# A ScalarE copy between the parts of the last pair's chain, in the halved feed-forward stages

## The chip, the cores and the metric

The kernel runs on one core of one Trainium2 chip. The metric is the device time of one execution in microseconds (us). Five engines work side by side and wait for each other through semaphores: TensorE (PE in the profile; PEld is its weight load) multiplies matrices, VectorE (DVE) and ScalarE (ACT) work on elements, GpSimd (POOL) and SyncE (SP) here mostly issue transfers (DMA). Each engine takes its own instructions strictly in the order in which they stand in its queue.

## The reference, cut to what matters

One decoder layer over 512 tokens of width 1024: a feed-forward half-step, a mixing stage with two kinds of attention, and a second feed-forward half-step. The change lies in the two half-steps alone:

```python
D_MODEL = 1024; SEQ = 512; D_FF = 2816

def swiglu_ffn(x, g, w_gate, w_up, w_down):
    h = rms_norm(x, g)
    return (jax.nn.silu(h @ w_gate) * (h @ w_up)) @ w_down

x = x + 0.5 * swiglu_ffn(x, ffn1_norm, ffn1_w_gate, ffn1_w_up, ffn1_w_down)
...                                   # attention, gates, output projection
x = x + 0.5 * swiglu_ffn(x, ffn2_norm, ffn2_w_gate, ffn2_w_up, ffn2_w_down)
```

All of it is in float32.

## The kernel before, in words

**Precision.** Every float32 operand is held as two parts, a high one (a ScalarE cast) and a low one (a VectorE subtraction of the high part from the source). One product is three matmuls (`mm3`, lines 147 to 149): high weights by high data, high weights by low data, low weights by high data. For a weight tile, `split_w` makes the parts: ScalarE casts `wh` on line 116, VectorE subtracts `wl` on line 123. So the third matmul of the first `mm3` of a product is the first that needs `wl`.

**Steps.** `ffn` writes its work as a list of steps. A step has weights to load, a `split` that makes their two parts, and a `run` that multiplies. The main loop takes the steps one after the other. At step i it first calls `look_ahead(i)`, which loads and splits the weights of the steps up to i + 2 (so at step i it is step i + 2 that is newly split), then empties the list `later`, and then calls `run` of step i. Between `ordered[0]` and `ordered[1]` the order of the instructions on ScalarE, VectorE and GpSimd is the order in which the Python code writes them; TensorE's order is written out for the whole kernel.

**Pairs.** The 22 tiles of 128 columns of the hidden width D_FF go in groups, (0, 4), (4, 10), (10, 16), (16, 22). From the fifth tile on, two tiles make a pair, and a pair's gate and up products are made by a scheme of seven products of half-size blocks in place of eight (steps A, s1, s2, b, s3, s4, d in `pair_steps`), at the price of sums of blocks made by VectorE. When the last product of a pair is done, `finish` puts a closure `begin` into `later`: the Silu (line 397), the product with it (398), and then what the down product needs.

**Halved down products.** In the groups of `HALVED` (two in the first half-step, three in the second: five places in the program) the down product has seven half-size products as well. Its moving operands are the blocks `b1`, `ta`, `tb`, `b2`, each as a high and a low part. `combine_first` makes `b1` and the first half of `ta` from the pair's first tile; `combine_second` (lines 260 to 276) makes the rest from the second tile `u`: `fb` and `fa` are VectorE's sums, `split_halves` casts (245) and subtracts (247). Of the last pair of a group this is done at once, the high parts of `tb`'s first half and `b2` first (267, 272), and it falls into the first steps of the down product. This is the chain of the title.

**The seven down steps** (`halved_steps`, twice per group, for two halves of the output) are, in TensorE's order: `run_1` (bank dA from `b1`; ScalarE then copies dA into dB, line 521), `run_5` (dD from `ta`'s first half), `run_6` (adds `tb`'s first half onto dB), `run_2` (adds `b2`'s first half onto dA), `run_7` (`ta`'s second half onto dB), `run_3` (dC), `run_4` (dB). Each has 18 matmuls of 256 columns: six `mm3`, and the two of the last pair come last, so that only the 13th to the 18th matmul of a product need the last pair's blocks. dD goes out through ScalarE copies `e` (513), in the very last group through VectorE (506).

Of the kernel before, what the change touches and what calls it, by code (L numbers as in the profile page):

```python
# [12 lines left out]
F32 = mybir.dt.float32  # L13
F32R = mybir.dt.float32r
AF = mybir.ActivationFunctionType
OP = mybir.AluOpType
# [4 lines left out]
T = 512  # L21
# [26 lines left out]
HT = T // 2  # L48
# [6 lines left out]
def tile_hybrid_layer(ctx: ExitStack, tc: tile.TileContext, a: dict):  # L55
    nc = tc.nc
    V, S, G, PE = nc.vector, nc.scalar, nc.gpsimd, nc.tensor
# [12 lines left out]
    def tmp_tile(name):  # L70
        return tmp.tile([P, T], F32, tag="t", name=name)
# [33 lines left out]
    first = None  # L105
# [93 lines left out]
    def ffn(n, nxt, parts=lambda d: [slice(0, T)]):  # L199
        wg, wu, wp, wd, wh_ = (a[f"w_{nm}{n}"] for nm in ("gate", "up", "pair", "down", "halves"))  # L200
        gi = 0 if n == 1 else 2
        with tc.tile_pool(name=f"ffn{n}", bufs=1) as ap, tc.tile_pool(name=f"halves{n}", bufs=1) as hp:
# [12 lines left out]
            def split_act(f, u, late):  # L215

                h, l = act_tiles(f)
                S.copy(h, u)
                if late:
                    S.mul(l, h.bitcast(F32), -1.0)  # L220
                    G.dma_start(l, u, accum_op=OP.add)
                else:
                    V.tensor_sub(l, u, h.bitcast(F32))

            def halves(q):
                lo = next(lo for lo, hi in GROUPS if lo <= 2 * q < hi)
                j = q - lo // 2
                if q not in act:
                    tiles = [ap.tile([P, 2 * T], F32R, tag=f"a{j}{i}", name=f"a{i}") for i in "hl"]
                    ta = stream(6 + j, F32R, "ta") if j < 2 else ap.tile([P, 2 * T], F32R, tag="a2t", name="ta")  # L230
                    b1 = ap.tile([P, T], F32R, tag=f"a{j}b", name="b1")
                    act[q] = dict(b2=[t[:, :T] for t in tiles], tb=[t[:, T:] for t in tiles],
                                  ta=[ta[:, :T], ta[:, T:]], b1=[b1[:, :HT], b1[:, HT:]])
                return act[q]

            def split_late(q, nm, src, cols):
                h, l = (t[:, cols] for t in halves(q)[nm])
                S.copy(h, src)
                S.mul(l, h.bitcast(F32), -1.0)
                G.dma_start(l, src, accum_op=OP.add)  # L240

            def split_halves(q, *which):
                t = halves(q)
                for nm, src, cols in which:
                    S.copy(t[nm][0][:, cols], src[:, cols])
                for nm, src, cols in which:
                    V.tensor_sub(t[nm][1][:, cols], src[:, cols], t[nm][0][:, cols].bitcast(F32))
# [12 lines left out]
            def combine_second(q, u, last):  # L260
                t = halves(q)
                fa, fb = t["fa"], tmp_tile("fb")
                first, second = slice(0, HT), slice(HT, T)
                V.scalar_tensor_tensor(fb[:, first], fa[:, first], -1.0, u[:, second], op0=OP.mult, op1=OP.subtract)
                if last:
                    for nm, src, cols in (("tb", fb, first), ("b2", u, slice(0, T))):
                        S.copy(t[nm][0][:, cols], src[:, cols])
                V.tensor_sub(fa[:, second], u[:, second], t["u1"][:, second])
                V.scalar_tensor_tensor(fb[:, second], fb[:, first], -1.0, u[:, first], op0=OP.mult, op1=OP.subtract)
                if last:  # L270
                    for nm, src, cols in (("tb", fb, first), ("b2", u, slice(0, T))):
                        V.tensor_sub(t[nm][1][:, cols], src[:, cols], t[nm][0][:, cols].bitcast(F32))
                    split_halves(q, ("ta", fa, second), ("tb", fb, second))
                    return []
                return [lambda nm=nm, src=src: split_late(q, nm, src, slice(0, T))
                        for nm, src in (("b2", u), ("tb", fb), ("ta", fa))]

            def activate(f, pg, pu, rb):
# [98 lines left out]
            def pair_steps(q, last, halved):  # L377
# [4 lines left out]
                t, raw = {}, {}  # L382
# [11 lines left out]
                def finish(f, gu):  # L394

                    def begin():
                        S.activation(gu[:, 0], gu[:, 0], AF.Silu)
                        V.tensor_mul(gu[:, 1], gu[:, 1], gu[:, 0])
                        if not halved:
                            return [lambda: split_act(f, gu[:, 1], not last)]  # L400
                        return (combine_second if f % 2 else combine_first)(q, gu[:, 1], last)

                    later.append((begin, last))

                def gu_tile():
                    return stream(2 + next(gu_at), F32, "gu").rearrange("p (m t) -> p m t", m=2)
# [41 lines left out]
                def run_s4(w):  # L448
                    product(t["C"], w, moving("b2", 1), False)
                    V.tensor_add(t["gu1"][:, :, HT:], view(t["C"]), view(t["p5"]))  # L450
                    finish(2 * q, t["gu1"])

                def run_d(w):
                    product(t["B"], w, moving("tb", 1), False)
                    S.mul(t["gu2"][:, :, :HT], view(t["B"]), -1.0)
                    finish(2 * q + 1, t["gu2"])
# [140 lines left out]
                return run  # L597

            steps = []
            later = deque()  # L600
            ordered = [None, None]
            gu_at = cycle(range(4))
            for lo, hi in GROUPS:
# [27 lines left out]
            def load():  # L631
                i, (key, f, src) = queue.pop(0)

                tag = max(sorted(free), key=lambda z: used[::-1].index(z) if z in used else len(used))
                free.remove(tag)
                used.append(tag)
                t = ap.tile([P, 1024], F32, tag=tag, name=tag) if tag in ("rd", "re", "rf") else raw_tile(tag)
                steps[i].raw[key] = t, tag
                nc.sync.dma_start(t[:, :f * P].rearrange("p (n m) -> p n m", n=f) if f else t, src)

            def look_ahead(i):

                for j in range(i, min(i + 1 + steps[i].ahead, len(steps))):
                    if j not in ws:
                        while queue and queue[0][0] <= j:
                            load()
                        ws[j] = steps[j].split()
                        free.update(steps[j].raw[z][1] for z in steps[j].frees)
                while queue and queue[0][0] <= i + 6 and free:
                    load()  # L650
# [4 lines left out]
            for i, st in enumerate(steps):  # L655
                if i == ordered[0]:
                    in_order.enter_context(tc.manual_schedule(engines={
                        mybir.EngineType.Activation, mybir.EngineType.DVE, mybir.EngineType.Pool}))
                look_ahead(i)
                while later:  # L660
                    item, urgent = later.popleft()
                    later.extendleft((z, urgent) for z in reversed(item() or ()))
                    if not urgent and i < ordered[1]:
                        break
                if i == ordered[1]:
                    in_order.close()
                st.run(ws[i])
                if rbs and combos:
                    for _ in range(2):
                        if next(combos, "end") == "end":  # L670
                            combos = None
                            free.add("rd")
                            break
# [3 lines left out]
    first = [[], []]  # L677
# [22 lines left out]
    gq = const.tile([P, 2], F32, name="gq")  # L700
    V.tensor_scalar(gq, hg[:, 0:2], -0.125, None, op0=OP.mult)
    ffn(1, lambda d, cols: (prep(d, 1), add_square(d)))


    with (tc.tile_pool(name="mix", bufs=1) as mp, ExitStack() as att_ctx,
# [255 lines left out]
        def dsa_keys():  # L961
            for t in range(NT):
                r = qk_scale(sd[0][:, t, 0], 1)
                V.tensor_scalar(sd[0][:, t], sd[0][:, t], r[:, 0:1], None, op0=OP.mult)
                S.copy(dvv[:, t, 0:64], sg[:, t, 0:64])
                V.tensor_sub(dvv[:, t, 64:128], sg[:, t, 0:64], dvv[:, t, 0:64].bitcast(F32))
            yield
            evac_split(transposed(lambda t: sd[0][:, t].rearrange("p a d -> p (a d)"), "ps_dk"), hg[:, 3:4], dkh, dkl)
# [80 lines left out]
        later = [dsa_keys(), forget()]  # L1049
# [146 lines left out]
        for g in range(2 * H):  # L1196
            q, k, bias = nq, nk, nb
# [69 lines left out]


    ffn(2, lambda d, cols: nc.sync.dma_start(a["y"][:, d, cols], x[d][:, cols]),
        lambda d: [slice(0, T)] if d < KD - 1 else [slice(0, T // 2), slice(T // 2, T)])  # L1270

# [79 lines left out]
```

## Time and profile before

| | |
|---|---|
| median of 3 runs | 1094.66 us (1093.4 to 1096.35) |
| the profiled execution, its own time | 1093.11 us |
| its span, from the first to the last instruction | 1091.4 us |
| what lies around the span | 1.71 us |
| PE busy | 1061.4 us, 97% of the span |
| PE weight loads | 980.7 us, 90% |
| DVE busy | 838.8 us, 77% |
| ACT busy | 662.4 us, 61% |
| POOL busy | 242.5 us, 22% |
| mean clock granted to TensorE | 0.993 of full speed |

How to read the rows that follow. A row of a timeline has the start and the duration in us, the engine, the line of the kernel, the operation, what it writes and reads, its shapes, and in brackets how long the engine was idle before it and what it waited for. Names stand without their numbers: `s` is a sum of weight blocks, `wh` and `wl` the two parts of a weight tile, `ah` and `al` those of the blocks `tb` and `b2`, `gu` a pair's gate and up result, `ra` to `rf` raw weight tiles. A row of waits has the total wait in us, how often, and the longest. A matmul's duration in a row is longer than the distance between the starts of two, since they overlap.

### The profile page before, as it was taken

The numbers are of one execution on the slowest core, as the hardware profiler recorded it, in microseconds if no ns is written. First come the engines' busy times: TensorE is split into PE (matmuls) and PEld (weight loads), VectorE is DVE, ScalarE is ACT, GpSimd is POOL, SyncE is SP. The second block draws the span as 40 slices with busy tenths as digits, with TensorE's granted clock in tenths as the row PEclk, the third lists the DMA queues.
The fourth block names the chain that finished last, engine by engine and source line by source line (L and its number), as shares of the span: only waits on it lengthen the run. The fifth ranks groups of instructions, "written<-read, shape, count | busy, mean of one in ns | idle before, by whom it ended". The sixth has DMA issues, their size and how long they took to land.

```text
span 1091.4 us, 19211 instructions
## 1 busy us (share of the span) xinstructions
PE 1061.4 (97%) x7330; PEld 980.7 (90%) x7330; DVE 838.8 (77%) x1375; ACT 662.4 (61%) x1096; POOL 242.5 (22%) x311
## 2 busy tenths in 40 slices
PE   8999999999999999999999999999999999999998
PEld 6889999999998889999878788788889999999998
DVE  6887888877867579986776676854877878787886
ACT  6736765755665665576866666444637655855763
POOL 1100210111000024267776661000101110110110
PEclk9999999999999999999999999999999999999999
DMA  7544754657442267723323321633555654656553
GB/s 234 144 154 108 158 137 140 139 142 183 109 107 89 78 145 173 214 89 106 79 60 115 116 68 49 196 100 82 116 158 125 139 158 122 144 135 173 121 121 108
DMA packets 55133, 140.04 MB, mean 128 GB/s; under 512 B 6392, under 2 KB 13944, under 8 KB 55040
## 3 DMA queue, kind: packets, MB, share of 16 engines
q1 hardware_dynamic: 39888, 110.22, 33.8%
q0 software_dynamic: 15008, 28.32, 14.6%
q8 instruction: 58, 0.95, 0.4%
q10 hardware_dynamic: 144, 0.26, 0.1%
q14 instruction: 35, 0.29, 0.1%
HBM read 104.94 MB, written 3.42 MB: 99 GB/s over the span
## 4 chain that ended last, share of the span: by engine, by line
PE 69%; DVE 11%; issue 8%; ACT 6%; POOL 4%; DMA 2%; SPq 0%; DVEq 0%; POOLq 0%; ACTq 0%
PE pB L148 4%; PE pB L147 4%; PE pB L149 4%; PE pA L148 3%; PE pA L147 3%; PE pA L149 3%; PE ps_f L147 3%; PE ps_f L148 3%; PE ps_f L149 3%; PE dB L147 2%; PE dB L148 2%; PE dB L149 2%; PE pD L148 2%; PE pD L149 2%; PE pD L147 2%
## 5 line engine op out<-in xcount | busy, mean ns | idle before, releaser
L123 DVE TENSOR_TENSOR wl<-s,wh 128x1024 fp32r<-128x1024 f32 (+1 forms) x84 | 94.6, 1126 | 39.5 <-ACT wh L116 39.5
L116 ACT CAST wh<-s 128x1024 fp32r<-128x1024 f32 (+1 forms) x84 | 81.8, 973 | 61.9 <-PE pC L148 31.1
L147 PE MATMUL ps_t<-wh,xh 128*128 128x256 f32 (+1 forms) x288 | 80.6, 280 | 0.0
L149 PE MATMUL pB<-tbh,wl 128*128 128x256 f32 x288 | 80.4, 279 | 0.0
L147 PE MATMUL pB<-tbh,wh 128*128 128x256 f32 x288 | 80.4, 279 | 0.0
L148 PE MATMUL pB<-tbl,wh 128*128 128x256 f32 x288 | 80.4, 279 | 0.0
L148 PE MATMUL ps_t<-wl,xh 128*128 128x256 f32 (+1 forms) x288 | 80.3, 279 | 0.0
L149 PE MATMUL ps_t<-wh,xl 128*128 128x256 f32 (+1 forms) x288 | 80.3, 279 | 0.0
L147 PE MATMUL ps_f<-xh,wh 128*128 128x512 f32 x152 | 60.5, 398 | 0.0
L149 PE MATMUL ps_f<-xh,wl 128*128 128x512 f32 x152 | 59.6, 392 | 0.0
L148 PE MATMUL ps_f<-xl,wh 128*128 128x512 f32 x152 | 59.6, 392 | 0.0
L147 PEld LDWEIGHTS ps_t<-wh,xh 128*128 128x128 f32 x288 | 54.3, 188 | 0.5
L148 PEld LDWEIGHTS ps_t<-wl,xh 128*128 128x128 f32 x288 | 54.3, 188 | 0.5
L1062 ACT ACTIVATE p<-p,mn 128x512 f32<-128x512 f32 (+1 forms) x64 | 36.0, 562 | 30.6 <-DVE mn L1060 30.1
L149 PEld LDWEIGHTS ps_t<-wh,xl 128*128 128x128 f32 x288 | 54.3, 188 | 0.0
L147 PEld LDWEIGHTS pB<-tbh,wh 128*128 128x128 f32 x288 | 54.1, 188 | 0.0
L149 PEld LDWEIGHTS pB<-tbh,wl 128*128 128x128 f32 x288 | 54.1, 188 | 0.0
L148 PEld LDWEIGHTS pB<-tbl,wh 128*128 128x128 f32 x288 | 54.1, 188 | 0.0
L240 POOL DMA_DIRECT2D b<-gu x10 | 8.7, 866 | 197.9 <-DVE rf L417 100.7
L1064 POOL TENSOR_SCALAR p<-p,rs 128x512 f32<-128x512 f32 (+1 forms) x64 | 39.1, 614 | 59.6 <-DVE rs L1063 59.2
L147 PE MATMUL dB<-ah,wh 128*128 128x256 f32 x120 | 37.0, 308 | 11.7 <-ACT dB L521 11.7
L515 POOL DMA_DIRECT2D xa<-e x16 | 19.1, 1193 | 124.8 <-ACT wh L116 115.8
(399 smaller groups left out, 4152.0 us busy)
## 6 DMA issues: line engine op xcount, KB each, us to landing
ra<-in_w_pair_dram SPq DMA_DIRECT2D x15, 512.0 KB, 3.7
rc<-in_w_pair_dram SPq DMA_DIRECT2D x15, 512.0 KB, 4.0
re<-in_w_pair_dram SPq DMA_DIRECT2D x12, 512.0 KB, 4.0
rf<-in_w_pair_dram SPq DMA_DIRECT2D x12, 512.0 KB, 3.7
rb<-in_w_pair_dram SPq DMA_DIRECT2D x12, 512.0 KB, 3.6
xa<-e POOLq DMA_DIRECT2D x16, 256.0 KB, 3.8
rd<-in_w_halves_dram SPq DMA_DIRECT2D x10, 384.0 KB, 3.8
al<-gu POOLq DMA_DIRECT2D x14, 256.0 KB, 5.3
```

The lines of the kernel that those rows point to most:

```text
L116: S.copy(wh[:, :f], raw[:, :f])
L123: V.tensor_sub(wl[:, :f], raw[:, :f], wh[:, :f].bitcast(F32))
L147: PE.matmul(out, lh, rh, start=start, stop=False, **more)
L148: PE.matmul(out, lh, rl, start=False, stop=False, **more)
L149: PE.matmul(out, ll, rh, start=False, stop=stop, **more)
L240: G.dma_start(l, src, accum_op=OP.add)
L515: return lambda: G.dma_start(xa[:, d:d + 2, half * HT:half * HT + HT], e, accum_op=OP.add)
L1062: S.activation(p, p, AF.Exp, bias=mn, scale=-1.0, accum_out=rs)
L1064: G.tensor_scalar(p, p, rs, 1.0, op0=OP.mult, op1=OP.mult)
```

## The change

For the second tile of the last pair of a halved group, `begin` goes into a new list `before`, which the loop empties ahead of `look_ahead`. `combine_second` does then only the Silu, its product and the first half of `fb`, and puts the closure `soon` into another new list, `after`, which the loop empties behind `run`. `soon` splits the first half of `tb` and the whole of `b2`, makes the second halves of `fa` and `fb`, and puts their split into `later`, where the next step takes it, after its own `look_ahead`. So the chain is in three parts: ahead of the first step's weight split, behind the first step's `run` (and so behind the copy from dA to dB), and behind the second step's weight split. No instruction is added or taken away; GpSimd's and SyncE's queues have the same rows in the same order, and so has TensorE's.

```diff
@@ combine_second
                 t = halves(q)
                 fa, fb = t["fa"], tmp_tile("fb")
-                first, second = slice(0, HT), slice(HT, T)
+                first, second, both = slice(0, HT), slice(HT, T), slice(0, T)
                 V.scalar_tensor_tensor(fb[:, first], fa[:, first], -1.0, u[:, second], op0=OP.mult, op1=OP.subtract)
+
+                def others():
+                    V.tensor_sub(fa[:, second], u[:, second], t["u1"][:, second])
+                    V.scalar_tensor_tensor(fb[:, second], fb[:, first], -1.0, u[:, first], op0=OP.mult, op1=OP.subtract)
+
+                def soon():
+                    split_halves(q, ("tb", fb, first), ("b2", u, both))
+                    others()
+                    later.append((lambda: split_halves(q, ("ta", fa, second), ("tb", fb, second)), True))
+
                 if last:
-                    for nm, src, cols in (("tb", fb, first), ("b2", u, slice(0, T))):
-                        S.copy(t[nm][0][:, cols], src[:, cols])
-                V.tensor_sub(fa[:, second], u[:, second], t["u1"][:, second])
-                V.scalar_tensor_tensor(fb[:, second], fb[:, first], -1.0, u[:, first], op0=OP.mult, op1=OP.subtract)
-                if last:
-                    for nm, src, cols in (("tb", fb, first), ("b2", u, slice(0, T))):
-                        V.tensor_sub(t[nm][1][:, cols], src[:, cols], t[nm][0][:, cols].bitcast(F32))
-                    split_halves(q, ("ta", fa, second), ("tb", fb, second))
+                    after.append(soon)
                     return []
-                return [lambda nm=nm, src=src: split_late(q, nm, src, slice(0, T))
+                others()
+                return [lambda nm=nm, src=src: split_late(q, nm, src, both)
                         for nm, src in (("b2", u), ("tb", fb), ("ta", fa))]
@@ finish, in pair_steps
-                    later.append((begin, last))
+                    if last and halved and f % 2:
+                        before.append(begin)
+                    else:
+                        later.append((begin, last))
@@ the list of steps
-            later = deque()
+            before, later, after = deque(), deque(), deque()
@@ the main loop
+                while before:
+                    before.popleft()()
                 look_ahead(i)
                 while later:
...
                 st.run(ws[i])
+                while after:
+                    after.popleft()()
```

ScalarE, at the first of the five places (the others read alike): the last pair's Silu, the weight casts of the down product's third and fourth step (`wh<-s_1448`, `wh<-rf`), the casts of the last pair's blocks, and the copy from dA to dB. Before:

```order
L455 ACTIVATE gu<-pB 128x2x256
L116 CAST wh<-s_1448 128x768
L397 ACTIVATE gu<-gu 128x512
L267 CAST ah<-fb 128x256
L267 CAST ah<-gu 128x512
L245 CAST ta<-fa 128x256
L245 CAST ah<-fb 128x256
L521 COPY dB<-dA 128x512
L116 CAST wh<-rf 128x768
```

and of the change (its line numbers are 4 to 7 higher here):

```order
L462 ACTIVATE gu<-pB 128x2x256
L401 ACTIVATE gu<-gu 128x512
L116 CAST wh<-s_1448 128x768
L528 COPY dB<-dA 128x512
L245 CAST ah<-fb 128x256
L245 CAST ah<-gu 128x512
L116 CAST wh<-rf 128x768
L245 CAST ta<-fa 128x256
L245 CAST ah<-fb 128x256
```

The Silu stands ahead of the weight cast, the copy ahead of the four casts of blocks, and the second weight cast ahead of the last two of them.

VectorE at the same place, from the Silu's product (`gu<-gu`) to the low part of the fourth step's weights (`wl<-rf`) and the block subtractions. Before:

```order
L123 TENSOR_TENSOR wl<-s_1448,wh 128x768
L398 TENSOR_TENSOR gu<-gu 128x512
L264 SCALAR_TENSOR_TENSOR fb<-fa,gu 128x256
L268 TENSOR_TENSOR fa<-gu 128x256
L269 SCALAR_TENSOR_TENSOR fb<-fb,gu 128x256
L272 TENSOR_TENSOR al<-fb,ah 128x256
L272 TENSOR_TENSOR al<-gu,ah 128x512
L247 TENSOR_TENSOR ta<-fa,ta 128x256
L247 TENSOR_TENSOR al<-fb,ah 128x256
L477 TENSOR_TENSOR s_1448<-s_1448,rf 128x768
L123 TENSOR_TENSOR wl<-rf,wh 128x768
```

and of the change:

```order
L402 TENSOR_TENSOR gu<-gu 128x512
L264 SCALAR_TENSOR_TENSOR fb<-fa,gu 128x256
L123 TENSOR_TENSOR wl<-s_1448,wh 128x768
L247 TENSOR_TENSOR al<-fb,ah 128x256
L247 TENSOR_TENSOR al<-gu,ah 128x512
L267 TENSOR_TENSOR fa<-gu 128x256
L268 SCALAR_TENSOR_TENSOR fb<-fb,gu 128x256
L484 TENSOR_TENSOR s_1448<-s_1448,rf 128x768
L123 TENSOR_TENSOR wl<-rf,wh 128x768
L247 TENSOR_TENSOR ta<-fa,ta 128x256
L247 TENSOR_TENSOR al<-fb,ah 128x256
```

The low part of the third step's weights moved behind the Silu's product and the first `fb`; the second halves of `fa` and `fb` moved behind the first two block subtractions, and the last two block subtractions behind the fourth step's weights.

## The prediction

> **What bounds the kernel now.** I read the page first, for the busiest engine, and then who that engine waits for.
>
> ```profile
> PE 1061.4 (97%) x7330; PEld 980.7 (90%) x7330; DVE 838.8 (77%) x1375; ACT 662.4 (61%) x1096; POOL 242.5 (22%) x311
> ```
>
> TensorE is busy for 97% of the span, so only its idle time and its pace are to be had. The view of waits, for TensorE alone, begins:
>
> ```profile
> PE dB L147 <- ACT dB L521: 11.7, 5, 2.3
> PE pt L1071 <- POOL p L1064: 2.0, 3, 1.2
> ```
>
> The first row is six times the second: five stops of up to 2.3 us, before the first matmul into dB, for ScalarE's copy of dA into dB. They are the five places of the change. I take the second of them; TensorE's timeline there:
>
> ```profile
> 231.17 0.27 PE L149 MATMUL dD<-ta,wl 128*128 128x256 f32 x1
> 233.79 0.43 PE L147 MATMUL dB<-ah,wh 128*128 128x256 f32 x1 [2.34 <-ACT dB L521]
> ...
> 237.54 0.28 PE L147 MATMUL dA<-ah,wh 128*128 128x256 f32 x1
> ...
> 239.65 0.28 PE L147 MATMUL dB<-ta,wh 128*128 128x256 f32 x1
> ```
>
> The dA product (18 matmuls) takes 239.65 - 237.54 = 2.11 us, 0.117 a matmul. So dB could have begun at 231.17 + 0.12 = 231.29, and the stop costs 233.79 - 231.29 = 2.50 us (the row's 2.34 counts from the end of the last matmul). The dB product behind it takes 237.54 - 233.79 = 3.75 us, which is 1.64 more than the same 18 matmuls in dA. The granted clock says why (columns: window, its length, busy us of PE, PEld, DVE, ACT, POOL, then the clock):
>
> ```profile
> 138.42:141.83 3.41, 2.21 (x19) 2.00 (x18) 2.96 (x6) 1.85 (x5) 0.00 (x0) 1.00 0.37 112
> 230.58:233.99 3.41, 1.07 (x9) 0.86 (x8) 3.38 (x10) 2.27 (x6) 0.00 (x0) 1.00 0.02 5
> 233.99:237.40 3.41, 3.41 (x17) 3.41 (x17) 2.74 (x4) 2.20 (x4) 0.00 (x0) 0.50 0.18 25
> 527.54:530.95 3.41, 1.83 (x15) 1.39 (x14) 3.02 (x6) 2.81 (x5) 3.33 (x8) 1.00 0.98 251
> 530.95:534.36 3.41, 3.41 (x29) 3.33 (x28) 2.95 (x10) 3.11 (x8) 3.32 (x4) 1.00 0.45 105
> ```
>
> After a window in which TensorE was idle for 3.41 - 1.07 = 2.34 us it ran 3.41 us at half speed. The first place (first row), whose stop is cut by the edge of a window into pieces of about 1.2, has no such stretch (its rows stand below), nor has the window behind the worst one elsewhere (the last two rows: 1.58 idle, then 1.00).
>
> **The change, part by part.** No instruction is added; what moves is the order on ScalarE and VectorE. So I set the new order with the old rows' durations. ScalarE before, at this place:
>
> ```profile
> 228.31 0.59 ACT L455 ACTIVATE gu<-pB 128x512 f32<-128x512 f32 x1
> 228.80 0.82 ACT L116 CAST wh<-s 128x768 fp32r<-128x768 f32 x1
> 229.52 0.63 ACT L397 ACTIVATE gu<-gu 128x512 f32<-128x512 f32 x1
> 231.72 0.40 ACT L267 CAST ah<-fb 128x256 fp32r<-128x256 f32 x1 [1.56 <-DVE fb L264]
> 232.03 0.61 ACT L267 CAST ah<-gu 128x512 fp32r<-128x512 f32 x1
> 232.55 0.40 ACT L245 CAST ta<-fa 128x256 fp32r<-128x256 f32 x1
> ...
> 233.16 0.57 ACT L521 COPY dB<-dA 128x512 f32<-128x512 f32 x1
> 233.67 0.82 ACT L116 CAST wh<-rf 128x768 fp32r<-128x768 f32 x1
> ```
>
> and VectorE:
>
> ```profile
> 229.66 0.96 DVE L123 TENSOR_TENSOR wl<-s,wh 128x768 fp32r<-128x768 f32 x1 [0.80 <-ACT wh L116]
> 230.53 0.69 DVE L398 TENSOR_TENSOR gu<-gu 128x512 f32<-128x512 f32 x1
> 231.26 0.42 DVE L264 SCALAR_TENSOR_TENSOR fb<-fa,gu 128x256 f32<-128x256 f32 x1
> 231.60 0.42 DVE L268 TENSOR_TENSOR fa<-gu 128x256 f32<-128x256 f32 x1
> ...
> 232.67 0.69 DVE L272 TENSOR_TENSOR al<-gu,ah 128x512 fp32r<-128x512 f32 x1
> 233.28 0.42 DVE L247 TENSOR_TENSOR ta<-fa,ta 128x256 fp32r<-128x256 f32 x1
> ...
> 233.95 0.95 DVE L477 TENSOR_TENSOR s<-s,rf 128x768 f32<-128x768 f32 x1
> 234.82 0.95 DVE L123 TENSOR_TENSOR wl<-rf,wh 128x768 fp32r<-128x768 f32 x1
> ```
>
> A result is taken up 0.04 us after it is done (product ends at 231.22, `fb` starts at 231.26); an independent instruction starts a little before its forerunner ends: 0.72 us behind a weight cast, 0.31 behind a cast of 256, 0.52 behind one of 512, 0.34 behind a VectorE sum of 256, 0.61 behind one of 512, 0.87 behind one of 768.
>
> *The Silu goes ahead of the weight cast.* It starts at 228.31 + 0.59 + 0.04 = 228.94 and ends at 229.57. VectorE, idle for 0.80 us just there, takes the product at 229.61 (to 230.30) and `fb` at 230.34 (to 230.76): 0.92 us earlier than before.
>
> *The weight cast, and the copy behind it.* The cast starts 0.53 behind the Silu, at 229.47, and ends at 230.29; the copy follows at 229.47 + 0.72 = 230.19 and ends at 230.76, 2.97 us earlier than before and 0.53 ahead of the slot of 231.29 that TensorE has for dB. dA must be done by then; its last matmul stands before the 18 of dD, so about 2.1 us ahead of 231.29. The stop for the copy is gone.
>
> *What is late next, first.* `wl<-s` now stands behind product and `fb`: 230.34 + 0.34 = 230.68 to 231.64, where it ended at 230.62. The third matmul of dB (231.29 + 0.23 = 231.52) needs it; with 0.06 from an end to a matmul (copy's end 233.73, dB 233.79) that is 231.70, a stop of **0.18 us**. The last pair's blocks are needed only by the 13th matmul (232.9): `ah<-fb` is cast at 230.80, once `fb` is done, and `al<-fb` follows `wl<-s` at 231.55, done at 231.97. About 0.9 us of older pairs' matmuls cover it; without that cover TensorE would wait as long as it now does for `al`.
>
> *What is late next, second.* VectorE goes on: `al<-gu` at 231.89, `fa` at 232.50, `fb` at 232.84, the sum `s` at 233.17, `wl<-rf` at 234.04, done at 234.99. That is only 0.78 us earlier than before. dA now begins at 231.29 + 0.18 + 2.11 = 233.57, its third matmul is due at 233.80 and must wait for 234.99 + 0.06 = 235.05: a new stop of **1.25 us**. Between the ends "hidden" (0) and "`wl<-rf` as late as before" (2.03) I take 1.25, since each step of that chain has its row. Before, the slow dB product had covered this tile.
>
> *The step after.* ScalarE's casts of the second halves wait for `fa` and `fb` (232.96 and 233.30), two `e` copies and the cast of `rd` follow, as before:
>
> ```profile
> 234.40 1.07 ACT L513 ACTIVATE e<-dD 128x512 f32<-128x512 f32 x2
> 235.37 0.82 ACT L116 CAST wh<-rd 128x768 fp32r<-128x768 f32 x1
> ```
>
> With 0.30 + 0.97 + 0.82 behind 233.30 the cast ends at 235.39; VectorE reaches `wl<-rd` at 234.04 + 0.87 + 2 x 0.34 = 235.59 and ends at 236.55. The next product (`ta`'s second half) begins at 233.57 + 2.11 + 1.25 = 236.93 and needs it at 237.16: hidden by 0.6 us. Its start was 239.65, so this place gains **2.72 us**. Behind it VectorE and ScalarE wait for TensorE again, and all that follows, transfers with it, moves as one; no load or accumulating transfer changes its place in its queue.
>
> *The clock.* The new stops leave about 1.1 us between modelled ends of matmuls, less than the 1.58 that brought no slow stretch. I take full speed. The Trainium skill bears on this ("TensorE: Matmul & The Clock Gate", section "What's actually happening"): the clock falls to half after at least one idle window of about 3.4 us and is given back after a busy one. The half-speed stretch of 3.41 us agrees with its window; the condition does not, since 2.34 us of idleness in a window were enough here. By the page alone the stops could not be the cause, and the slow stretches would stay.
>
> *The other places.* dB's old start and the next product's old start:
>
> ```profile
> 142.97 0.39 PE L147 MATMUL dB<-ah,wh 128*128 128x256 f32 x1 [2.34 <-ACT dB L521]
> ...
> 147.27 0.28 PE L147 MATMUL dB<-ta,wh 128*128 128x256 f32 x1
> ...
> 875.81 0.58 PE L147 MATMUL dB<-ah,wh 128*128 128x256 f32 x1 [2.33 <-ACT dB L521]
> ...
> 881.61 0.28 PE L147 MATMUL dB<-ta,wh 128*128 128x256 f32 x1
> ...
> 968.13 0.58 PE L147 MATMUL dB<-ah,wh 128*128 128x256 f32 x1 [2.34 <-ACT dB L521]
> ...
> 973.85 0.28 PE L147 MATMUL dB<-ta,wh 128*128 128x256 f32 x1
> ...
> 1060.36 0.58 PE L147 MATMUL dB<-ah,wh 128*128 128x256 f32 x1 [2.35 <-ACT dB L521]
> ...
> 1066.09 0.28 PE L147 MATMUL dB<-ta,wh 128*128 128x256 f32 x1
> ```
>
> At place two the new start is 236.93, 3.14 behind dB's old one; the same chain puts the others at 146.11, 878.95, 971.27 and 1063.50: gains of 1.16 (no slow stretch there before), 2.66, 2.58 and 2.59. The last place has one more piece on VectorE:
>
> ```profile
> 1062.26 1.28 DVE L506 SCALAR_TENSOR_TENSOR xa<-dD,xa 128x512 f32<-128x512 f32 x2
> 1063.46 0.95 DVE L123 TENSOR_TENSOR wl<-rd,wh 128x768 fp32r<-128x768 f32 x1
> ```
>
> These 1.20 us stand ahead of `wl<-rd`, which then ends 1.20 us later than at place two, 0.64 too late (237.75 + 0.06 against 237.16): 2.59 - 0.64 = 1.95.
>
> **Sum:** 1.16 + 2.72 + 2.66 + 2.58 + 1.95 = 11.07 us. The profiled execution took 1093.11 us, span 1091.4 and 1.71 around it, and would take 1082.0. It lies 1.55 below the median of the runs; from the median I predict 1094.66 - 11.07 = **1083.6 us**.
>
> **The rivals.**
>
> *The half speed stays* at four places, whether the shorter stops still bring it or something else did. For it: the first place shows that the condition depends on where a window begins. Against it: every slow stretch followed a window with over 2 us idle, and none came elsewhere. The excess of dB's products over 2.11 us is worth 1.64 + 1.58 + 1.50 + 1.51 = 6.23 (next product's start less dB's, less 4.22); the gain falls to 4.84, 1089.8 us. By the page's rule it comes out here too.
>
> *VectorE's chain is not earlier:* `wl<-rf` ends at 235.77 as before. For it: VectorE has no idle time from 230.53 to there. Against it: the 0.80 us before `wl<-s` is taken away. 0.78 less at each place: gain 7.2, 1087.5.
>
> *No new stop:* everything is saved, 5 x 2.50 + 6.23, less 5 x 0.18: 17.8, 1076.9. Against it stands the row of `wl<-rf`; it would have to be done 1.2 us sooner.
>
> *Slower:* one stop has become two, and idle time in two neighbouring windows drops the clock in both. From about 1 us idle per window on, each place would pay the stops (1.43, once 0.64 more) and two slow stretches of about 1.56: 7.8 + 15.6 = 23.4 against 5 x 2.50 + 6.23 = 18.7 now, 4.7 slower, 1099.4. Against it: 1.58 us idle in one window did nothing.
>
> **How the numbers follow.** Forecast 0.67, VectorE not earlier 0.11, half speed stays 0.11, no new stop 0.07, slower 0.04. The forecast's own range is 1081 to 1086 (a quarter of a microsecond at each stop, and the spread of the runs). To hold eight in ten the range takes in the second and third case: 1079.5 to 1090. A measurement of this kernel tells 0.3%, 3.3 us, from no change. The half-speed case lies near that edge, and with a late VectorE inside it: of its 0.11 I count 0.07 as the same. Faster 0.67 + 0.11 + 0.04 + 0.07 = 0.89, same 0.07, slower 0.04.
>
> **What would show it.** Right: the wait of dB's L147 for ScalarE's copy is gone from TensorE's waits; in its place stand waits of dA's L149 for `wl` of about 1.1 us, five times, with `wl` ending 0.8 us earlier against the pair's last product; the clock is 1.00 behind all five places; the dB product takes 2.1 to 2.3 us. Wrong: half-speed windows at the same places; a stop at dB's 13th matmul for `ah` or `al`; a new stop at the `ta` product at places one to four; or a copy that starts later than dD ends.

## The result, and the profile after

The changed kernel takes 1083.57 us (median of 4 runs, 1082.64 to 1084.4) against 1094.2 before (4 runs), a ratio of 0.990 with the interval 0.9881 to 0.9918. It is faster by 1.0%, and 1083.6 was forecast. In a second comparison it took 1082.8 against 1093.47, ratio 0.9902 (0.9885 to 0.9918). The profiled execution took 1084.4 us, its span is 1082.6.

TensorE's waits in the profile after:

```profile
PE dA L149 <- DVE wl L123: 4.9, 5, 1.0
PE pt L1082 <- DVE kl L737: 1.8, 3, 1.1
...
PE dB L149 <- DVE wl L123: 0.4, 1, 0.4
```

The 11.7 us for ScalarE's copy are gone. In their place stand five waits of 1.0 us for the low part of the fourth step's weights, and one of 0.4 at the last place. TensorE's timeline at place two, which answers to the rows of before:

```profile
231.99 0.28 PE L149 MATMUL dD<-ta,wl 128*128 128x256 f32 x1
232.11 0.28 PE L147 MATMUL dB<-ah,wh 128*128 128x256 f32 x1
232.22 0.28 PE L148 MATMUL dB<-al,wh 128*128 128x256 f32 x1
232.43 0.38 PE L149 MATMUL dB<-ah,wl 128*128 128x256 f32 x1
...
234.40 0.28 PE L147 MATMUL dA<-ah,wh 128*128 128x256 f32 x1
234.52 0.27 PE L148 MATMUL dA<-al,wh 128*128 128x256 f32 x1
235.78 0.39 PE L149 MATMUL dA<-ah,wl 128*128 128x256 f32 x1 [0.98 <-DVE wl L123]
...
237.76 0.28 PE L147 MATMUL dB<-ta,wh 128*128 128x256 f32 x1
```

ScalarE's copy there:

```profile
230.96 0.58 ACT L528 COPY dB<-dA 128x512 f32<-128x512 f32 x1
```

It ends at 231.54, 0.57 us before dB's first matmul at 232.11. dB follows dD without a stop; its third matmul comes 0.21 us behind the second where 0.12 is usual; dA's third comes 1.26 behind the second. From dD's last matmul to the `ta` product it is 237.76 - 231.99 = 5.77 us, before 239.65 - 231.17 = 8.48: a gain of 2.71. Why dA waits stands on VectorE:

```profile
230.36 0.69 DVE L402 TENSOR_TENSOR gu<-gu 128x512 f32<-128x512 f32 x1 [0.73 <-ACT gu L401]
231.09 0.43 DVE L264 SCALAR_TENSOR_TENSOR fb<-fa,gu 128x256 f32<-128x256 f32 x1
231.43 0.95 DVE L123 TENSOR_TENSOR wl<-s,wh 128x768 fp32r<-128x768 f32 x1
...
233.91 0.95 DVE L484 TENSOR_TENSOR s<-s,rf 128x768 f32<-128x768 f32 x1
234.78 0.95 DVE L123 TENSOR_TENSOR wl<-rf,wh 128x768 fp32r<-128x768 f32 x1
```

From the Silu's product to the start of `wl<-rf` VectorE works without a break, 4.42 us, and `wl<-rf` ends at 235.73, 0.05 before dA's third matmul. The windows of 3.41 us around it (PE busy is the second column, the clock the third from the end):

```profile
234.42:237.83 3.41, 2.43 (x21) 2.23 (x20) 3.26 (x6) 2.96 (x6) 0.00 (x0) 1.00 0.24 66
237.83:241.25 3.42, 3.42 (x31) 3.42 (x30) 3.21 (x5) 1.68 (x2) 0.00 (x0) 1.00 0.69 219
...
428.98:432.39 3.41, 3.41 (x28) 3.24 (x27) 3.38 (x10) 3.03 (x6) 2.27 (x2) 1.00 0.53 107
432.39:435.80 3.41, 3.41 (x10) 2.66 (x9) 3.41 (x13) 0.00 (x0) 1.56 (x3) 0.50 0.86 207
```

0.98 us of idle time brings no half speed here, nor does the same stop at the other four places. But there is one half-speed stretch in the attention stage that the execution before did not have, behind a window in which the rows show no idle time at all. It is taken up at the end.

The five places, measured from the first matmul of dD to that of dC in both timelines (at place two 229.18 to 241.74 before, 229.99 to 239.85 after):

| place | before, us | after, us | gain | forecast |
|---|---|---|---|---|
| 1 | 11.00 | 9.91 | 1.09 | 1.16 |
| 2 | 12.56 | 9.86 | 2.70 | 2.72 |
| 3 | 12.49 | 9.90 | 2.59 | 2.66 |
| 4 | 12.42 | 9.92 | 2.50 | 2.58 |
| 5 | 12.46 | 10.54 | 1.92 | 1.95 |
| sum | | | 10.80 | 11.07 |

The profiled spans differ by less, 8.8 us: the execution after reached the first place 1.32 us later (dD at 139.69, before at 138.37), ahead of all that the change touches, and paid the stretch at 432 us. The rest, about 1 us the other way, lies between the places and was not followed up.

### The profile page after: what moved, and what is told of

The parts are those of the page before. It is cut to its first block, busy times and chain, and to the rows that moved or that the text cites. A ratio compares the mean times of both kernels' runs of the same rounds, so it can differ in the third digit from the quotient of the medians.

```text
span 1082.6 us, 19216 instructions
## 1 busy us (share of the span) xinstructions
PE 1059.2 (98%) x7330; PEld 976.7 (90%) x7330; DVE 837.3 (77%) x1375; ACT 663.1 (61%) x1096; POOL 243.4 (22%) x311
## 4 chain that ended last, share of the span: by engine, by line
PE 71%; DVE 12%; issue 8%; ACT 5%; POOL 3%; DMA 2%; SPq 0%; DVEq 0%; POOLq 0%; ACTq 0%
PE pB L147 4%; PE pB L149 4%; PE pB L148 4%; PE ps_f L147 3%; PE pA L147 3%; PE pA L148 3%; PE pA L149 3%; PE ps_f L148 3%; PE ps_f L149 3%; PE ps_t L147 2%; PE ps_t L149 2%; DVE wl L123 2%; PE ps_t L148 2%; PE dB L149 2%; PE dB L147 2%
## 5 line engine op out<-in xcount | busy, mean ns | idle before, releaser
L1087 DVE TENSOR_TENSOR pl<-pt,ph 128x512 fp32r<-128x512 f32 (+1 forms) x64 | 31.1, 486 | 20.6 <-ACT ph L1086 20.0
```

The costliest lines, as they stand in the source:

```text
L1087: V.tensor_sub(pl[:, sl], pt[:, sl], ph[:, sl].bitcast(F32))
```

## The experiments

All ratios are against the kernel before, run beside it. The edits are shown against the change, that of the filled stop against the kernel before, and that of the spread small matmuls against the kernel named there; `...` marks lines left out.

**The copy alone.** The chain begins where it did before, behind `look_ahead`; the rest stays behind the copy.

```diff
-                    if last and halved and f % 2:
-                        before.append(begin)
-                    else:
-                        later.append((begin, last))
+                    later.append((begin, last))
```

> The chain begins where it did before (Silu behind the third step's weight cast); only its rest is put behind the copy, and its last split behind the fourth step's weights. Theory (stops plus clock): the copy is out of the way, but VectorE's chain gains nothing, so dA's third matmul waits for its weights about 2.2 us at each place (idle about 1.95 in the rows). At full speed that is 0.3 to 0.4 us less a place than before; the time is about 1092.5 if that idle time still brings half speed at four places, about 1086 if it brings it at none. Rival 'the copy's place is all of it': 1083.6, no wait of dA.

It took 1093.16 us, ratio 0.9997 (0.9985 to 1.001): no gain. Its first place, in its waits and windows:

```profile
PE dA L149 <- DVE wl L123: 9.5, 5, 1.9
```

```profile
143.38:146.80 3.42, 1.52 (x11) 1.23 (x11) 3.37 (x7) 3.06 (x7) 0.00 (x0) 1.00 0.00 0
146.80:150.21 3.41, 3.41 (x17) 3.41 (x17) 2.23 (x4) 1.57 (x4) 0.00 (x0) 0.50 0.65 190
```

The stop for the copy is gone and has come back 2.1 us later as one of 1.9 for `wl`, with the half-speed stretch behind it, at four of the five places of this execution. That the copy's place is all of it is refuted: VectorE's chain has to start earlier too.

**The Silu alone.** `begin` stays ahead of `look_ahead`, and the chain is one piece again, as in the lines that the change took out.

```diff
                 if last:
-                    after.append(soon)
+                    for nm, src, cols in (("tb", fb, first), ("b2", u, slice(0, T))):
+                        S.copy(t[nm][0][:, cols], src[:, cols])
...
+                    split_halves(q, ("ta", fa, second), ("tb", fb, second))
                     return []
```

> The whole chain goes ahead of the third step's weight split in one piece, with the copy behind it as before. Theory: ScalarE makes the copy at about the same time as before (end about 233.5 in the time of place two), and the low part of the weights comes later still (about 234.05), so TensorE stops about 2.3 us for the copy and 0.3 more for the weights: no gain, 1094 (1092 to 1097), half-speed stretches as before. Rival 'the gain is the Silu taken into VectorE's idle time': 1087 or less.

1094.83 us, ratio 1.001 (1.000 to 1.002), and TensorE waits as before:

```profile
PE dB L147 <- ACT dB L525: 10.7, 5, 2.2
```

So neither of these two parts of the change is worth anything without the other.

**Two parts in place of three.** The last split goes with the rest, ahead of the fourth step's weights.

```diff
-                    later.append((lambda: split_halves(q, ("ta", fa, second), ("tb", fb, second)), True))
+                    split_halves(q, ("ta", fa, second), ("tb", fb, second))
```

> The change with its third part undone: the last split (second halves of ta and tb) stands with the rest behind the copy, ahead of the fourth step's weights. Theory: two VectorE subtractions of 0.34 us come ahead of wl<-rf, the stop at dA grows by 0.68 us a place, from 0.98 idle to about 1.66; the time is 1083.6 + 3.4 = 1087.0 at full speed, and if 1.66 idle in one window is enough for half speed, about 1.6 us more for each place, up to 1095. Rival 'the third part is without effect, the copy decides': 1083.6.

1092.05 us, ratio 0.9985 (0.9971 to 1.0). The third part of the change, which I had priced at 3.4 us at full speed, is worth 8.5 by the rows of the five places (together 58.7 us against 50.1 with the change). TensorE at place two, then the windows of places two and three:

```profile
235.34 0.39 PE L147 MATMUL dA<-ah,wh 128*128 128x256 f32 x1 [0.64 <-ACT wh L116]
235.57 0.28 PE L148 MATMUL dA<-al,wh 128*128 128x256 f32 x1
236.81 0.38 PE L149 MATMUL dA<-ah,wl 128*128 128x256 f32 x1 [0.96 <-DVE wl L123]
```

```profile
234.08:237.49 3.41, 1.81 (x13) 1.40 (x12) 3.00 (x6) 3.41 (x8) 0.00 (x0) 1.00 0.00 0
237.49:240.90 3.41, 3.41 (x18) 3.41 (x17) 2.28 (x4) 1.58 (x2) 0.00 (x0) 0.50 0.73 234
875.79:879.20 3.41, 2.03 (x16) 1.62 (x14) 3.27 (x7) 2.77 (x6) 0.00 (x0) 1.00 0.00 0
879.20:882.61 3.41, 3.19 (x27) 3.19 (x28) 2.85 (x5) 2.48 (x4) 0.00 (x0) 1.00 0.62 186
```

The idle time is 1.60 us, where 1.66 was expected, though in two pieces: the high part `wh`, which I had left out, comes 0.64 late as well, since its cast now stands behind two casts that wait for VectorE. And 1.60 us in one window are enough: half speed follows at three of five places. Where the window's edge leaves only 1.38 in one window (place three) it does not. The executions differ accordingly: four of ten took 1089.5 to 1089.6 us, the others up to 1094.7.

**The stop filled.** The kernel before, with a second dD product into a bank that nothing reads, in the time in which TensorE waits.

```diff
                     product("D", w, "ta", 0, True)
+                    if s == 0:
+                        t["X"] = psum.tile([P, T], F32, tag="pv", name="dX")
+                        product("X", w, "ta", 0, True)
```

> The kernel before, with 18 more matmuls of 256 columns in front of dB at each of the five places: the dD product a second time, into a bank that nothing reads. They only fill 2.1 of the 2.5 us for which TensorE waits. Theory: the stop leaves 0.4 us, the clock stays at full speed behind all five places, and the time falls by the four slow stretches, 6.2 us, to about 1088. Rival 'the half-speed stretches have another cause than the stop': 1094, and the stretches stay.

1088.53 us, ratio 0.9952 (0.9936 to 0.9968): 90 more matmuls make the kernel faster. Its wait row, and its span with the mean clock:

```profile
PE dB L147 <- ACT dB L521: 1.2, 5, 0.3
```

```profile
core 0: 1085.2 us, clock 1.000
```

The copy is as late as before; only the idle time is gone, and with it, in the profiled execution, every half-speed stretch. So the idle time of the stops causes those at the places. Of the seven executions three have a mean clock of 1.000; the others have 0.994 to 0.998, and where their stretches lie is not known.

**The sum behind the weights.** The change, with VectorE's sum of weight blocks behind `wl<-rf`.

```diff
-                    return split(raw["b"][0], add(t["s2"], t["s2"], raw["b"][0]))
+                    w = split(raw["b"][0])
+                    add(t["s2"], t["s2"], raw["b"][0])()
+                    return w
```

> The change, and VectorE's sum of weight blocks for the sixth down step (0.87 us) put behind wl<-rf instead of ahead of it. Theory: wl<-rf is VectorE's chain and nothing else, so the stop at dA falls from 0.98 to about 0.1 us. But the chain as a whole is as long: the weights of the product after it (wl<-rd) come no sooner, so 0.3 us of a new stop arises at places one to four, and at the last place all that was won (VectorE adds dD there first). Gain 0.55 x 4 = 2.2 us: 1081.4. Rival 'dA waits for something else': 1083.6.

1082.86 us, ratio 0.9902 (0.9883 to 0.992), the same as the change beside it. In the rows it does what was expected, here at the first place:

```profile
143.96 0.28 PE L147 MATMUL dA<-ah,wh 128*128 128x256 f32 x1
144.08 0.27 PE L148 MATMUL dA<-al,wh 128*128 128x256 f32 x1
144.47 0.39 PE L149 MATMUL dA<-ah,wl 128*128 128x256 f32 x1
...
146.45 0.28 PE L147 MATMUL dB<-ta,wh 128*128 128x256 f32 x1
...
148.85 0.28 PE L147 MATMUL dC<-ah,wh 128*128 128x256 f32 x1
```

dA has no idle time left, and its product runs 2.49 us where it ran 3.34 (2.11 is usual); `ta`'s product runs 2.40 us where it ran 2.10, a place takes 9.36 us instead of 9.91, and the last place waits as long as ever:

```profile
PE dB L149 <- DVE wl L123: 1.2, 1, 1.2
```

The 2.2 us do not show in the median of five runs. Three of these had a mean clock of 0.996 and one 0.999, against one below 1.000 among the four of the change beside it; where their stretches lay is known only of the profiled one (at 24 and 430 us, away from the places).

**TensorE's order of need.** The change, with VectorE's order after the first block subtraction set by when TensorE needs each result. The edit is shortened: `high` and `low` are the cast and the subtraction of one block.

```diff
                 def soon():
-                    split_halves(q, ("tb", fb, first), ("b2", u, both))
+                    high("tb", fb, first); high("b2", u, both); low("tb", fb, first)
                     others()
-                    later.append((lambda: split_halves(q, ("ta", fa, second), ("tb", fb, second)), True))
+                    later.append((then, True))
+                def then():
+                    low("b2", u, both); high("ta", fa, second); high("tb", fb, second)
+                    after.append(lambda: later.append((last_two, True)))     # last_two: the two low parts
...
-                    return split(raw["b"][0], add(t["s2"], t["s2"], raw["b"][0]))
+                    w = split(raw["b"][0])
+                    later.append((add(t["s2"], t["s2"], raw["b"][0]), True))
+                    return w
...
-                        Step(raw, [], split_b, run_2, "b"),
-                        Step(raw, [], lambda: split(raw["c"][0]), run_7, "c"),
+                        Step(raw, [], split_b, run_2),
+                        Step(raw, [], lambda: split(raw["c"][0]), run_7, "bc"),
```

(In `run_5` of the last group the two adds of dD go through `after` and `later` too.)

> The change, with VectorE's order after the first block subtraction set by when TensorE needs each result: second halves of fa and fb, wl<-rf, the low part of b2, the sum of weight blocks, wl<-rd, the low parts of the second halves, and at the last place the adds of dD after these. The raw weight tile of the sum is given free one step later. Theory: no stop of dA and of the product after it is left, 1.23 us less at each place and 0.62 more at the last: 1083.6 - 6.8 = 1076.8, the stop of 0.15 us in dB stays. Rival 'ScalarE is the bound there': wh<-rd comes late, stops at the ta product stay, about 1080.

1078.54 us, ratio 0.9864 (0.9849 to 0.9879), the fastest of all, 4.3 us below the change beside it. Each place now takes 8.67 to 8.72 us, so that the rows of the places give 4 x 1.2 + 1.86 = 6.7, as expected. One wait at dC is new, at the last place and behind the end of what the 6.7 counts:

```profile
PE dC L149 <- DVE wl L123: 0.4, 1, 0.4
```

```profile
1052.30 0.28 PE L147 MATMUL dC<-ah,wh 128*128 128x256 f32 x1
1052.42 0.27 PE L148 MATMUL dC<-al,wh 128*128 128x256 f32 x1
1053.07 0.38 PE L149 MATMUL dC<-ah,wl 128*128 128x256 f32 x1 [0.37 <-DVE wl L123]
...
1055.23 0.35 PE L147 MATMUL dB<-ah,wh 128*128 128x256 f32 x1
```

The dC product lasts 2.93 us there, 0.83 more than the usual 2.10, which leaves 5.9. The profiled executions of this kernel and of the change beside it, both without a half-speed stretch before their last matmul, differ by 5.8 us (spans 1076.5 and 1082.3). At place two VectorE still works without a break up to `wl<-rd`; what moved is only which results come first. Of this gain the medians show 4.3; what is missing was not followed up.

**The change again, and small matmuls.** The change run beside these:

> The change itself again, beside the others: 1083.6, five stops of about 1.0 us at dA for the low part of its weights, no half speed at the five places; where the mean clock is 0.998, one stretch in the attention stage near 432 us, worth 1.7 us.

As expected, 1082.8 us, five waits of 1.0, and in its profiled execution no half-speed stretch at all. For the stretch at 432 us, the kernel of the last experiment was run with the ten matmuls of 8 columns that make the forget gate's running sums spread between products:

```diff
             for t in range(NT):
+                if t:
+                    prod.run(MM)
                 for j in range(t + 1):
```

> The last kernel, and the ten matmuls of 8 columns for the forget gate's running sums (attention stage, near 430 us) no longer stand together but between products of 512 columns. Theory 'the clock counts work, not busy time': the half-speed stretch near 432 us, which comes in some executions though the rows show TensorE busy there, comes in none; the spread falls and the median by up to 0.9 us: 1076. Rival 'the stretch has to do with something else': the stretch stays in about half of the executions.

1080.15 us, ratio 0.9878 (0.9861 to 0.9896): not faster. The stretch near 432 is not in its profiled execution, which has one at 24 us instead; all four executions have a mean clock of 0.998, which does not tell where. The edit also changed the order of later products in the attention stage. It settles nothing. So the reverse, on the change itself:

```diff
-            for t in range(NT):
+            for t in [*range(NT), *range(NT)]:
                 for j in range(t + 1):
                     PE.matmul(pc[:, t * H:(t + 1) * H], trin if j == t else ones, lf[:, j], ...)
```

> The change, and the ten matmuls of 8 columns for the forget gate's running sums made twice in a row (the second time over the first, same result). Theory 'the clock counts work, not the busy time of the rows': some 4 to 5 us of matmuls of 8 columns stand together, so wherever the window's edge falls, one window has little work in it, and a half-speed stretch follows near 432 to 437 us in every execution: mean clock 0.998 or lower in each, where the change itself has 1.000 in part of its executions. Rival 'those stretches come from something else': they come in some executions and not in others, as before.

1087.89 us, ratio 0.9942 (0.9919 to 0.9964), 4 to 5 us above the change, of which about 2.2 are the ten more matmuls. The twenty small matmuls stand from 428.90 to 433.44 us, and around them the windows read:

```profile
430.69:434.10 3.41, 3.41 (x29) 3.28 (x29) 3.38 (x11) 1.11 (x2) 2.31 (x3) 1.00 0.45 80
434.10:437.51 3.41, 3.41 (x10) 2.64 (x9) 3.41 (x13) 0.00 (x0) 2.08 (x2) 0.50 0.99 228
```

Busy for the whole window, and half speed behind it; the three executions have 0.997, 0.996 and 0.995, none is at full speed. That fits the theory. It is not proof for each execution, since a second stretch, at 24 us, and a half-speed end behind the last matmul, which costs no time, can make up part of these clocks.

## Why the prediction was right, point by point

*The copy.* Forecast to end 0.53 us before TensorE is free for dB; it ended 0.57 before dB's first matmul, and there was no wait for it. The two experiments with one half of the change each show that both steps named, the Silu ahead of the weight cast and the copy ahead of the block casts, are needed.

*What is late next, first.* 0.18 us forecast at dB's third matmul. At place two the third matmul comes 0.21 - 0.12 = 0.09 late and the whole product lasts 2.29 where 2.11 is usual, 0.18 more; at the others it lasts 2.36 to 2.37, up to 0.26 more and a little above the 2.1 to 2.3 forecast. Small either way.

*What is late next, second.* 1.25 us forecast at dA's third matmul; the dA product lasts 3.34 to 3.36 us where 2.11 is usual, 1.24. This term decides the result, and it came from setting the new order with the old rows' starts and durations. VectorE's chain measured 4.42 us from product to `wl<-rf`, 4.43 in the working. That the wait hangs on VectorE's order is shown: with the sum behind `wl<-rf` the product's excess falls from 1.24 to 0.38 us.

*The step after.* Hidden at places one to four, 0.64 forecast at the last, where the `ta` product lasted 2.74 instead of 2.10.

*The clock.* Forecast at full speed behind all five places, and so it is. Of 18.7 us lost at the places before, 6.2 were booked to the clock; filling the stops without removing them gave back 4.9 of the median. By the rule of the Trainium skill ("TensorE: Matmul & The Clock Gate", section "What's actually happening"), an idle window of some 3.4 us, read as a window without any work, the stretches should have had another cause and stayed. The filled stop decides against it; the length of the stretch, 3.41 us, agrees with that page.

*The rivals.* "Half speed stays" was nearer than its 0.11 looked: with the third part undone, 1.60 us in one window bring it back, where the change has 0.98. I took the 1.58 us of one window of the attention stage for the safe side. At the places the limit lies below that or right at it, between 1.38 and 1.59, so the forecast was safe by the size of its stops and not by this reason. "VectorE's chain is not earlier" is what the copy alone gives, at 1093 and not 1087.5, since the half speed comes with it: I priced these two as separate, and they come together. The slower case, two windows at half speed at each place, was not seen: the first of the two stops leaves no idle time in the rows, and the second 0.98 us in one window.

*The median.* The forecast took 1094.66 as the start; more runs of the kernel before, 41 in three comparisons, have a median of 1093.47, with mean clocks of 0.990 (four runs, 1095.3 us on average) to 0.996 (1090.3). So the gain of the medians, 10.6 and 10.7 us, is close to the places' 10.8, and its exactness at 1083.6 is partly luck: the start taken was 0.46 us above the median that the kernel before had in the end (1094.2), the gain forecast was 0.44 too large, and the two cancel.

## What to carry to other kernels

When a copy or a cast ends a stall, lay out the whole queue of the next engine in the new order with the old rows' durations: the next stop and its size stand there, and moving only the instruction that is named in the wait may give nothing. Price a stall of TensorE with the slow matmuls that follow it, and keep the idle time in any 3.4 us well below 1.4 us, counting matmuls of a few columns as idle; a stop cut below that gains more than the length that is cut off. When several results of one engine are waited for, order them by when TensorE takes each up, down to the third matmul.

## What the runs showed of the hardware that was not expected

The half speed follows windows of 3.41 us whose edges lie at another place in each execution. In the profiled execution of the kernel before, the stretches at the last four places begin at 233.99, 875.70, 967.86 and 1060.02 us, 188, 27 and 27 times 3.4133 us apart; in the other profiled executions with more than one stretch their starts lie whole multiples apart too. At the places, in all eleven profiled executions, 1.38 us and less of idle time in one window brought none, 1.59 and more (15 windows) did. So the kernel before had four such stretches in its profiled execution, and by the mean clocks of its runs (0.990 to 0.996) an estimated two to six in others, depending on where the edges fall. Its runs spread from 1090.3 to 1096.4 us; those of the change spread from 1081.6 to 1084.4.

Away from the places idle time alone does not sort the windows: 1.58 us (kernel before, 527.54) and 1.67 (second profiled execution of the change, 1075.33, at its end) brought none, 1.17 near 21 us did. What TensorE has to multiply sorts them better. Of the windows at full speed in the eleven executions, every one in which matmuls with fewer than 2400 columns in total begin was followed by half speed (12 windows), and none with more than 3250 (3401 windows; the median of all is 7424). Between these numbers both occur, 14 with and 10 without; some rows are missing in the traces, and matmuls cut by an edge are counted whole.

So a window can be full in the rows and still count as idle. The ten matmuls of 8 columns take 2.15 us, and whether half speed follows goes by the window's edge. In five of the nine executions with these ten together one window holds them all, and in four of these five the stretch came; in the four where an edge cuts them (2.01 us and less in one window) it did not. 4.4 us of them, 2.6 in one window, brought it in the execution profiled with their number doubled.

The stretch at 24 us lies behind a window with 1.17 to 1.18 us of idle time and the eight matmuls of one column that follow it (the sums of squares of the first norm). It came in the five executions where at least 1.99 us of these two together lie in one window, and not in the six where an edge leaves at most 1.80. In the second profiled execution of the change the window has as much idle time, 1.16 us, but only part of these matmuls, 1.75 us with them, and no half speed followed. So they count as idle too, as far as these executions show.
